# Latents before queries: another order of projections in a mixer, and a third query buffer

## The chip, the cores and the metric

The kernel runs on one core of a Trainium2 chip, in float32. The metric is the device time of one execution in microseconds; the median of several runs counts.

## The reference, cut to what matters

One inference step of a backbone with two layers, on 128 context tokens and 256 latent tokens of width 1024, plus 128 cached context tokens that the latent tokens may read. Layer 0 has mixers A and B, layer 1 has mixers C and D; each is followed by a SwiGLU FFN. The change is in layer 1 alone:

```
cq, ckv, kpe, qd, kd, vd = split(h @ w_in, (384, 256, 32, 512, 256, 256))
qc  = rms_norm(cq) @ w_q_up                  # 8 heads x (64 + 32)
ckv = rms_norm(ckv)
qd, kd = rms_norm per head                   # 8 and 4 heads x 64
kc, vc = split(ckv @ w_kv_up), kpe joined to kc
oc = softmax(qc kc^T) vc                     # mixer C, 8 heads
od = softmax(qd kd^T) vd                     # mixer D, 8 heads on 4 kv heads
y  = concat(oc, od) @ w_out
```

Context tokens read themselves only; latent tokens read latent and cached tokens, with a rotation of queries and keys.

## The kernel before, in words

Tokens form three tiles of 128. The normed and modulated input of a layer lies transposed in SBUF as a high and a low part (`hH`, `hL`), and each weight is split likewise: ScalarE rounds it (`wh`, L122), VectorE subtracts (`wl`, L123). A product is then three matmuls (`mm3`, L127 to L129). `proj_all` projects all three tiles: its weights come in four quarters of 256 rows, and each quarter takes one of three raw buffers and one of three split buffers, in the order of the program.

PSUM has eight banks in this stage: four in the pool `ps` (`pst`), three in `pj` (`pjt`), one apart (`psa`). A projection of three tiles takes three banks. Projections of D's keys and values (columns 1184 to 1695 of `w_in`, begun in the boundary behind the FFN of layer 0 and handed over as `acc0`), of C's query latents (0 to 383) and of C's key/value latents with the rotated key (384 to 671) go to `pj`; that of D's queries (672 to 1183) goes to `ps`, where the attentions' scores go, too. The banks of `pj` also hold the transposes of keys (`tk`), of C's query latents (`tc`) and of its key latents (`tl`), and the expansions (`vn`, `kn` in `kv_up`; `qu`, `tqc` in `q_up`).

What empties the banks: `evac_dkv` squares the keys on ScalarE (L1274), sums on VectorE (L1276), takes the power -1/2 on GpSimd (L110), and the product L1287 is the last read of the bank. `evac_cq` copies and squares a tile's latents (L1354, L1355), transposes, scales and splits them; it uses two working buffers `u2` of three. `evac_dq` squares, rotates and transposes D's queries into `qD`, a buffer of kind `qS`; `q_up` writes its two halves into two more buffers of that kind, of which there are two.

The order is made by a list scheduler when the program is built: each instruction has its place in the program as its priority, and `with ahead(name)` moves that place forward by `AHEAD[name]` instructions, or back if the number is negative. Engines then take what is ready by priority. Loads of weights carry a lead of 1500. In the program, layer 1's mixer is: project D's queries; empty keys and values (`evac_dkv`); cached keys (`d_ctx`); empty D's queries; C's query latents (200 back); C's cached latents and key/value latents (400 back); `kv_up` (30 ahead); D's attention (100 ahead); `q_up` (1000 ahead); C's attention (400 ahead); the first half of the output projection (1500 ahead). An attention has five stages (the context tokens, then four pairs of heads), and a stage's scores and exponentials stand ahead of the weighted sums of the stage before.

Of the kernel before, what the change touches and what calls it, by code (L numbers as in the profile page):

```python
# [28 lines left out]

AHEAD = {"w": 1500, "w0": -700, "lv0": 1000, "lv1": 800, "attA": 1500, "attC": 400, "attD": 100, "fin": 500, "qs": -1500,  # L30
         "ada": -400, "ada_step": -500, "of0": -500, "of1": 1500, "ho0": 300, "ho1": 300, "gb": 100, "ib": -60,
         "kvup": 30, "cq": -200, "dctx": -100, "lat": -400, "chain": -700, "qup": 1000, "rope": 1000, "adav": -500,
         "of2": -200, "adav1": -100}

ADA = (([(0, 2), (0, 3), (0, 4)], [(0, 5, 0), (1, 0, 1), (1, 1, 0), (1, 2, 1), (1, 3, 0), (1, 4, 1)]), ([], [(1, 5, 0)]))
# [6 lines left out]
def tile_backbone_step(ctx, tc, I, O):  # L42
# [33 lines left out]
    @contextmanager  # L76
    def ahead(part, more=0):
        with tc.high_priority(offset=AHEAD[part] + more):
            yield
# [271 lines left out]
    def tok(t):  # L351
        return slice(t * P, (t + 1) * P)
# [3 lines left out]
    def proj_parts(src, n, bank=None):  # L356
        acc, ws = {}, {}

        def load(u, *a, **kw):
            ws[u] = wload(src(slice(u * 256, (u + 1) * 256)), 2, n, *a, **kw)  # L360

        def part(t, u):
            if t not in acc:
                acc[t] = (bank or pjt)(f"pj{t}")
            hi, lo = ws[u]
            for k in range(2):
                kk = 2 * u + k
                mm3(acc[t][:, :n], hH[:, kk, tok(t)], hL[:, kk, tok(t)], hi[:, k, :], lo[:, k, :],
                    kk == 0, kk == KD - 1)

        return acc, part, load

    def proj_all(w, c0, n, bank=None):
        acc, part, load = proj_parts(lambda ks: w[ks, c0:c0 + n], n, bank)
        for u in range(4):
            load(u)
            for t in range(3):
                part(t, u)
        return acc

    def proj_tm(w, c0, n, evac):
        acc = proj_all(w, c0, n)
        for t in range(3):
            evac(t, acc[t])
# [233 lines left out]

    def inv_sums(M, A, sm, nm, sink, n):
        if A.sink:  # L620
            es = M.sm.tile([P, n], F32, tag=f"es{n}", name="es")
            nc.vector.tensor_tensor(out=es.rearrange("p (a b) -> p a b", a=2), in0=nm, in1=sink, op=ALU.add)
            nc.scalar.activation(es, es, AF.Exp)
            nc.vector.tensor_tensor(out=sm, in0=sm, in1=es, op=ALU.add)
        rd = M.sm.tile([P, n], F32, tag=f"rd{n}", name="rd")
        nc.vector.reciprocal(out=rd, in_=sm)
        return rd


    def pair_1(M, i, A):  # L630
        pr = [M.tile("pr", F32).rearrange("p (t k) -> p t k", t=2) for _ in range(2)]
        mx = M.sm.tile([P, 2, 2], F32, tag="mx", name="mx")
        sm = M.sm.tile([P, 4], F32, tag="sm", name="sm")
        nm = M.sm.tile([P, 2, 2], F32, tag="nm", name="nm")
        heads = slice(2 * i, 2 * i + 2)
        for qt in range(2):
            s_ = [pst("s")[:, :NTOK] for _ in range(2)]
            A.s(s_, i, qt)
            for a in range(2):
                nc.vector.tensor_reduce(out=mx[:, qt, a:a + 1], in_=s_[a], op=ALU.max, axis=AX.X)  # L640
            neg_max(A, nm[:, qt], mx[:, qt], heads, 1 + qt)
            for a in range(2):
                nc.scalar.activation(pr[a][:, qt, :], s_[a], AF.Exp, bias=nm[:, qt, a:a + 1],
                                     scale=score_scale(A, 2 * i + a, 1 + qt),
                                     accum_out=sm[:, 2 * qt + a:2 * qt + a + 1])
        sink = C["sink"][:, heads].unsqueeze(1).to_broadcast([P, 2, 2]) if A.sink else None
        rd = inv_sums(M, A, sm, nm, sink, 4)
        for qt in range(2):
            for a in range(2):
                nc.gpsimd.tensor_scalar(out=pr[a][:, qt, :], in0=pr[a][:, qt, :],  # L650
                                        scalar1=rd[:, 2 * qt + a:2 * qt + a + 1], scalar2=1.0, op0=ALU.mult, op1=ALU.mult)
        return pr

    def evac(eng, out, in_):
        if eng:
            nc.vector.tensor_copy(out=out, in_=in_)
        else:
            nc.scalar.activation(out, in_, AF.Copy)
# [86 lines left out]
    def rope_apply(M, x, nh, hd, tab, tt, dst, dup, tag="t2"):  # L745
        q = hd // 4
        t2f = M.tile(tag, F32)[:, 0:nh * hd].rearrange("p (h d) -> p h d", h=nh)
        xv = x.rearrange("p h (b k q) -> p h b k q", b=2, k=2)
        t2 = t2f.rearrange("p h (b k q) -> p h b k q", b=2, k=2)
        sv = tab[:, tt, 1, :].rearrange("p (b k q) -> p b k q", b=2, k=2)  # L750
        for k in range(2):
            nc.gpsimd.tensor_tensor(out=t2[:, :, :, k, :], in0=xv[:, :, :, 1 - k, :],
                                    in1=sv[:, :, k, :].unsqueeze(1).to_broadcast([P, nh, 2, q]), op=ALU.mult)
        nc.vector.tensor_tensor(out=x, in0=x, in1=tab[:, tt, 0, :].unsqueeze(1).to_broadcast([P, nh, hd]), op=ALU.mult)
        if dup:
            for d, sl in dst:
                n = sl.stop - sl.start
                nc.vector.tensor_tensor(out=d, in0=x[:, sl].unsqueeze(2).to_broadcast([P, n, 2, hd]),
                                        in1=t2f[:, sl].unsqueeze(2).to_broadcast([P, n, 2, hd]), op=ALU.add)
        else:  # L760
            nc.vector.tensor_tensor(out=dst, in0=x, in1=t2f, op=ALU.add)


    def dups(M, nh):
        r = []
        for h0 in range(0, nh, 4):
            n = min(4, nh - h0)
            r.append((M.tile("t2", F32)[:, 0:n * P].rearrange("p (h a d) -> p h a d", h=n, a=2), slice(h0, h0 + n)))
        return r
# [19 lines left out]
    def turn_k(ds, kT, tk, bank=pst):  # L789
        for d, sl in ds:  # L790
            n = sl.stop - sl.start
            tp = bank("tk").rearrange("p (h t) -> p h t", h=4)
            for i in range(n):
                nc.tensor.transpose(tp[:, i, :], d[:, i].rearrange("p a d -> p (a d)"), ident)
            for i in range(0, n, 2):
                evac(i, kT[i // 2][:, :, tk], tp[:, i:i + 2, :])
# [443 lines left out]
    def mixer_cd(ps1, acc0):  # L1240
        w = I["w_in_cd"][0]
        SC_D = 64 ** -0.5
        SC_C = 96 ** -0.5
        es = ExitStack()
        M = Slots(es, {"m4": (4, 1152), "u2": (3, 512), "t2": (5, 512), "one": (1, 0), "m8": (3, 2048), "qS": (2, 1536),
                       "pr": (4, 768), "pt": (6, 512), "sc": (1, 0)})
        vD = M.one.tile([P, 4, 4, 64], F32, name="vD")
        scl = {}
# [16 lines left out]
        def d_ctx():  # L1265
            kcx = dups(M, 4)
            for i in range(2):
                dma(out=kcx[0][0][:, :, i, :], in_=I["cache_d_k"][0, 0])
            dma(out=vD[:, 3], in_=I["cache_d_v"][0, 0])
            turn_k(kcx, kD, slice(384, 512), pjt)  # L1270

        def head_ss(acc, nh):
            sq = M.tile("t2", F32)[:, 0:nh * 64].rearrange("p (h d) -> p h d", h=nh)
            nc.scalar.activation(sq, acc.rearrange("p (h d) -> p h d", h=nh), AF.Square)  # L1274
            ss = M.sm.tile([P, 8], F32, tag="ssd", name="ssd")
            nc.vector.tensor_reduce(out=ss[:, :nh], in_=sq, op=ALU.add, axis=AX.X)  # L1276
            return ss
# [17 lines left out]
        def evac_dq(t, acc):  # L1295
            qn = M.tile("t2", F32).rearrange("p (h d) -> p h d", h=8)
            nc.scalar.activation(qn, acc.rearrange("p (h d) -> p h d", h=8), AF.Copy)
            ss = head_ss(acc, 8)
            if t:
                rope_apply(M, qn, 8, 64, tbq, t - 1, qn, False)  # L1300
            else:
                nc.vector.tensor_tensor(out=qn, in0=qn, in1=C["gdq"].unsqueeze(1).to_broadcast([P, 8, 64]), op=ALU.mult)
            turn_q(qn, qD, tok(t))
            with ahead("qs"):
                query_scale("D", t, ss, 1.0 / 64, SC_D)
# [115 lines left out]
        kT = [t8(F32, f"kT{i}") for i in range(2)]  # L1421
        latH, latL = [M.tile("m4", F32R)[:, 0:1024].rearrange("p (k n) -> p k n", k=2) for _ in range(2)]
        cqH, cqL = [M.tile("m4", F32R).rearrange("p (k n) -> p k n", k=3) for _ in range(2)]
        acc1 = proj_all(w, 672, 512, pst)
        for t in range(3):
            evac_dkv(t, acc0[t])
        d_ctx()
        for t in range(3):
            evac_dq(t, acc1[t])
        with ahead("cq"):  # L1430
            proj_tm(w, 0, 384, evac_cq)
        with ahead("lat"):
            c_ctx_()
            proj_tm(w, 384, 288, evac_ckv)
        with ahead("kvup"):
            vC = kv_up()
        with ahead("attD"):
# [98 lines left out]
```

## Time and profile before

| | us |
|---|---|
| median of 3 runs | 1082.47 |
| lowest, highest | 1077.73, 1084.74 |
| the profiled execution | 1080.16 |
| its span, first to last instruction | 1078.3 |
| TensorE busy | 1023.6 (95%) |
| VectorE busy | 657.7 (61%) |
| ScalarE busy | 440.5 (41%) |
| GpSimd busy | 121.2 (11%) |

The span and all rows below are of the profiled execution, which lies 1.9 us above its span and 2.3 below the median. In the rows PE is TensorE's matmuls, PEld its weight loads, DVE VectorE, ACT ScalarE, POOL GpSimd, SP the queue that issues the DMAs; L with a number is a line of the kernel. An operation is written as output<-inputs. In rows of time, the first number is the start in us from the span's start, the second how long it took; idle time ahead of it and what ended it stand in brackets.

### The profile page before, as it was taken

The page shows a single profiled execution, that of the slowest core. Times are in us where ns is not written, and L with a number is a line of the kernel's source. Part 1 is how long each engine was busy: PE and PEld are TensorE (multiplying, and loading weights), DVE is VectorE, ACT ScalarE, POOL GpSimd, SP SyncE. Part 2 cuts the span into 40 slices and gives each one's busy share as a digit, 9 for nine tenths or more (in the row PEclk, how much of TensorE's full clock was granted, in tenths as well). Part 3 has the DMA queues.
Part 4 walks back from the last instruction along what each step waited for, and adds up shares of the span by engine and source line. Part 5 has one row for each costly group of instructions (what it writes and reads, how often), then busy time and mean ns, then how long its engine had stood idle before and what let it go on. Part 6 is the DMA issues. An engine that isn't in the chain of part 4 may idle for free.

```text
span 1078.3 us, 15811 instructions
## 1 busy us (share of the span) xinstructions
PE 1023.6 (95%) x6105; PEld 865.2 (80%) x6105; DVE 657.7 (61%) x1110; ACT 440.5 (41%) x776; POOL 121.2 (11%) x166
## 2 busy tenths in 40 slices
PE   5999999997899999999999998979899999999995
PEld 4889877565799899897688776665689999998885
DVE  2589767455897477377247867656499464443337
ACT  2376746333443333232134457555163333332231
POOL 0021201210300000000001243122130000000004
PEclk8999999999999999999999999989999999999998
DMA  9873254457257777766663621144136464543331
GB/s 306 261 229 96 84 194 148 128 166 254 79 176 229 262 205 234 233 202 224 219 198 105 188 66 61 34 156 157 40 114 198 122 192 137 164 129 129 126 117 59
DMA packets 114353, 173.12 MB, mean 161 GB/s; under 512 B 9419, under 2 KB 82150, under 8 KB 114278
## 3 DMA queue, kind: packets, MB, share of 16 engines
q1 hardware_dynamic: 113526, 171.78, 50.7%
q8 instruction: 48, 0.79, 0.3%
q10 hardware_dynamic: 752, 0.34, 0.1%
q14 instruction: 27, 0.22, 0.1%
HBM read 167.84 MB, written 4.24 MB: 160 GB/s over the span
## 4 chain that ended last, share of the span: by engine, by line
PE 75%; DVE 9%; DMA 8%; issue 3%; ACT 2%; POOL 2%; SPq 0%; DVEq 0%; ACTq 0%; POOLq 0%
PE pf L129 10%; PE pf L128 10%; PE pf L127 10%; PE o L127 6%; PE o L128 6%; PE o L129 6%; DMA ar<-in_w_ada 4%; PE pj L129 3%; PE pj L127 3%; PE pj L128 3%; PE ada_acc L203 3%; DVE wl L123 2%; PE hs L883 2%; PE s L722 2%; PE ov L679 1%
## 5 line engine op out<-in xcount | busy, mean ns | idle before, releaser
L123 DVE TENSOR_TENSOR wl<-wr,wh 128x1024 fp32r<-128x1024 f32 (+4 forms) x200 | 235.9, 1182 | 239.9 <-ACT wh L122 237.1
L122 ACT ACTIVATE wh<-wr 128x1024 fp32r<-128x1024 f32 (+4 forms) x200 | 202.4, 1015 | 345.0 <-PE pf L128 123.5
L129 PE MATMUL pf<-hH,wl 128*128 128x384 f32 x688 | 232.7, 338 | 0.0
L127 PE MATMUL pf<-hH,wh 128*128 128x384 f32 x688 | 232.4, 338 | 0.0
L128 PE MATMUL pf<-hL,wh 128*128 128x384 f32 x688 | 232.4, 338 | 0.0
L129 PEld LDWEIGHTS pf<-hH,wl 128*128 128x128 f32 x688 | 129.4, 188 | 3.1 <-issue 3.1
L128 PEld LDWEIGHTS pf<-hL,wh 128*128 128x128 f32 x688 | 129.4, 188 | 2.5 <-issue 2.5
L127 PEld LDWEIGHTS pf<-hH,wh 128*128 128x128 f32 x688 | 129.4, 188 | 2.3 <-issue 2.2
L127 PE MATMUL o<-wh,aH 128*128 128x512 f32 (+1 forms) x280 | 101.3, 362 | 0.4 <-DVE a L1182 0.4
L128 PE MATMUL o<-wl,aH 128*128 128x512 f32 (+1 forms) x280 | 101.2, 361 | 0.4 <-DVE wl L123 0.4
L129 PE MATMUL o<-wh,aL 128*128 128x512 f32 (+1 forms) x280 | 101.0, 361 | 0.0
L129 PE MATMUL pj<-wh,hL 128*128 128x512 f32 (+3 forms) x240 | 88.9, 372 | 1.9 <-POOL hL L344 1.7
L127 PE MATMUL pj<-wh,hH 128*128 128x512 f32 (+3 forms) x240 | 89.2, 376 | 0.4 <-DVE vT L174 0.2
L261 DVE SCALAR_TENSOR_TENSOR part<-ar,cT,part 128x512 f32<-128x512 f32 x112 | 80.4, 747 | 13.7 <-DMA ar<-in_w_ada 13.6
L128 PE MATMUL pj<-wl,hH 128*128 128x512 f32 (+3 forms) x240 | 88.7, 370 | 0.0
L110 POOL TENSOR_TENSOR ve<-ve,nhalf 128x1 f32<-128x1 f32 x12 | 7.0, 585 | 631.7 <-DVE ve L530 370.2
L127 PEld LDWEIGHTS o<-wh,aH 128*128 128x128 f32 x280 | 52.9, 189 | 10.1 <-issue 1.4
L129 PEld LDWEIGHTS o<-wh,aL 128*128 128x128 f32 x280 | 52.8, 188 | 9.2 <-issue 1.2
L128 PEld LDWEIGHTS o<-wl,aH 128*128 128x128 f32 x280 | 52.9, 189 | 8.8 <-DVE wl L123 0.7
L129 PEld LDWEIGHTS pj<-wh,hL 128*128 128x128 f32 x240 | 45.1, 188 | 12.0 <-POOL hL L344 2.6
L127 PEld LDWEIGHTS pj<-wh,hH 128*128 128x128 f32 x240 | 44.8, 188 | 9.7 <-issue 1.9
L128 PEld LDWEIGHTS pj<-wl,hH 128*128 128x128 f32 x240 | 45.2, 188 | 7.8 <-issue 1.0
(325 smaller groups left out, 1511.5 us busy)
## 6 DMA issues: line engine op xcount, KB each, us to landing
ar<-in_w_ada SPq DMA_DIRECT2D x80, 512.0 KB
wr<-in_w_ffn_down SPq DMA_DIRECT2D x44, 512.0 KB
wr<-in_w_ffn_gate SPq DMA_DIRECT2D x40, 512.0 KB
wr<-in_w_ffn_up SPq DMA_DIRECT2D x40, 512.0 KB
wr<-in_w_in_ab SPq DMA_DIRECT2D x18, 512.0 KB
ar<-in_w_ada SPq DMA_DIRECT2D x32, 256.0 KB
wr<-in_w_out SPq DMA_DIRECT2D x16, 512.0 KB
wr<-in_w_in_ab SPq DMA_DIRECT2D x16, 256.0 KB
```

The costliest lines, as they stand in the source:

```text
L110: nc.gpsimd.tensor_tensor(out=out, in0=v, in1=nhalf[:, :n], op=ALU.pow)
L122: nc.scalar.activation(hi, raw, AF.Copy)
L123: nc.vector.tensor_tensor(out=lo, in0=raw, in1=hi.bitcast(F32), op=ALU.subtract)
L127: nc.tensor.matmul(out, lh, rh, start=start, stop=False)
L128: nc.tensor.matmul(out, lh, rl, start=False, stop=False)
L129: nc.tensor.matmul(out, ll, rh, start=False, stop=stop)
L203: nc.tensor.matmul(acc[32 * g:32 * g + 32], st, src[:, :, g * P:(g + 1) * P], start=start, stop=stop, tile_position=(0, 32 * g))
L261: nc.vector.scalar_tensor_tensor(out=dst, in0=raw[:, j], scalar=sc, in1=dst, op0=ALU.mult, op1=ALU.add)
L679: nc.tensor.matmul(ov[64 * a:64 * a + 64], A.v(kc + 1, 2 * i + a), pt[a, kc], start=(kc == 0), stop=(kc == 2))
L722: nc.tensor.matmul(outs[a], q[rows], k[rows], start=True, stop=stop)
L883: nc.tensor.matmul(pp[:, b, :], Kc(b0 + b), Qc(b0 + b), start=True, stop=True)
```

## The change

The projection of D's queries and what follows from it (`d_ctx`, `evac_dq`) move behind C's two projections; C's projections lose the numbers that moved them back; and buffers of kind `qS` become three. Calls of the two attentions stay one after the other.

```diff
-         "kvup": 30, "cq": -200, "dctx": -100, "lat": -400, "chain": -700, "qup": 1000, "rope": 1000, "adav": -500,
+         "kvup": 30, "cq": 0, "dctx": -100, "lat": 0, "chain": -700, "qup": 1000, "rope": 1000, "adav": -500,
...
-        M = Slots(es, {"m4": (4, 1152), "u2": (3, 512), "t2": (5, 512), "one": (1, 0), "m8": (3, 2048), "qS": (2, 1536),
+        M = Slots(es, {"m4": (4, 1152), "u2": (3, 512), "t2": (5, 512), "one": (1, 0), "m8": (3, 2048), "qS": (3, 1536),
...
-        acc1 = proj_all(w, 672, 512, pst)
         for t in range(3):
             evac_dkv(t, acc0[t])
-        d_ctx()
-        for t in range(3):
-            evac_dq(t, acc1[t])
         with ahead("cq"):
             proj_tm(w, 0, 384, evac_cq)
         with ahead("lat"):
             c_ctx_()
             proj_tm(w, 384, 288, evac_ckv)
+        acc1 = proj_all(w, 672, 512, pst)
+        d_ctx()
+        for t in range(3):
+            evac_dq(t, acc1[t])
         with ahead("kvup"):
             vC = kv_up()
```

## Rows read from the trace of the kernel before

**Rows 1.** The chain that ended last, shares of the span by engine.

```profile
PE 75%; DVE 9%; DMA 8%; issue 3%; ACT 2%; POOL 2%; SPq 0%; DVEq 0%; ACTq 0%; POOLq 0%
```

**Rows 2.** Stretches: width; busy of PE, PEld, DVE, ACT, POOL; clock; DMA; GB/s.

```profile
608.00:625.00 17.00, 17.00 (x76) 13.69 (x75) 11.68 (x23) 4.79 (x9) 5.80 (x7) 1.00 0.63 196
625.00:637.00 12.00, 10.47 (x68) 10.20 (x67) 9.56 (x23) 6.61 (x15) 8.04 (x7) 1.00 0.19 48
637.00:693.00 56.00, 50.26 (x324) 36.59 (x323) 38.05 (x90) 36.96 (x102) 17.15 (x28) 1.00 0.16 49
693.00:714.00 21.00, 18.86 (x104) 16.38 (x104) 12.02 (x24) 9.95 (x18) 3.22 (x8) 1.00 0.33 112
714.00:723.00 9.00, 5.15 (x19) 4.17 (x20) 6.37 (x11) 4.26 (x13) 1.71 (x1) 0.62 0.58 192
723.00:753.00 30.00, 29.48 (x143) 17.86 (x141) 16.87 (x34) 16.91 (x42) 9.92 (x14) 1.00 0.47 158
753.00:771.00 18.00, 14.94 (x79) 9.92 (x79) 4.45 (x9) 6.70 (x16) 2.27 (x4) 1.00 0.01 1
```

**Rows 3.** TensorE's waits, 607 to 772: total us, times, longest.

```profile
PE tqc L1405 <- DVE nm L613: 3.4, 1, 3.4
...
PE tqc L1405 <- DVE u L761: 1.6, 2, 0.8
...
PE s L1416 <- DVE qS L1406: 1.0, 1, 1.0
```

**Rows 4.** Stretches of 2 us where the granted clock (last but two) is low.

```profile
716.00:718.00 2.00, 0.00 (x0) 0.00 (x0) 2.00 (x5) 0.00 (x0) 0.00 (x0) 0.50 0.81 250
...
722.00:724.00 2.00, 2.00 (x8) 1.58 (x8) 0.12 (x1) 2.00 (x11) 0.00 (x0) 0.82 0.43 123
```

**Rows 5.** TensorE in time: first and last of 21, 30 and 18 matmuls.

```profile
619.78 0.40 PE L127 MATMUL pj<-wh,hH 128*128 128x512 f32 x1
...
624.45 0.40 PE L129 MATMUL pj<-wh,hL 128*128 128x512 f32 x1
...
629.14 0.34 PE L127 MATMUL pj<-wh,hH 128*128 128x384 f32 x1
...
634.27 0.34 PE L129 MATMUL pj<-wh,hL 128*128 128x384 f32 x1
...
656.21 0.38 PE L127 MATMUL pj<-wh,hH 128*128 128x288 f32 x1
...
658.54 0.29 PE L129 MATMUL pj<-wh,hL 128*128 128x288 f32 x1
```

**Rows 6.** ScalarE, GpSimd and VectorE in time: emptying D's keys.

```profile
605.29 0.38 ACT L1274 ACTIVATE t<-pj 128x256 f32<-128x256 f32 x1 [0.34 <-PE pj L129]
...
610.09 1.37 POOL L110 TENSOR_TENSOR rds<-ssd,nhalf 128x4 f32<-128x4 f32 x1 [12.29 <-DVE ssd L1232]
...
611.49 0.42 DVE L1287 TENSOR_TENSOR t<-pj,rds 128x256 f32<-128x256 f32 x1 [0.30 <-POOL rds L110]
...
616.26 0.42 DVE L1287 TENSOR_TENSOR t<-pj,rds 128x256 f32<-128x256 f32 x1 [1.13 <-POOL rds L110]
...
621.25 0.43 DVE L1287 TENSOR_TENSOR t<-pj,rds 128x256 f32<-128x256 f32 x1 [1.19 <-POOL rds L110]
```

**Rows 7.** Last matmul of C's query latents; the stretch behind it.

```profile
644.94 0.34 PE L129 MATMUL pj<-wh,hL 128*128 128x384 f32 x1
...
645.00:656.00 11.00, 7.69 (x47) 4.15 (x45) 10.26 (x27) 8.53 (x25) 6.74 (x9) 1.00 0.32 109
```

**Rows 8.** TensorE in time: the first scores of D.

```profile
637.38 1.80 PE L722 MATMUL s<-k,qS 64*128 64x128 f32 x18
```

**Rows 9.** TensorE in time: D's last scores, C's first query expansion.

```profile
671.76 1.56 PE L722 MATMUL s<-k,qS 64*128 64x384 f32 x8
...
697.14 0.33 PE L127 MATMUL qu<-wh,m 128*128 128x384 f32 x1
```

**Rows 10.** The DMA queue in time: first weights of that expansion.

```profile
668.23 2.62 SPq L118 DMA_DIRECT2D wr<-in_c_w_q_up x2
```

## The prediction

> **What bounds the kernel now.** I read the chain that ended last first: three quarters of the span lie on TensorE [rows 1], so a change pays only where it removes or creates idle TensorE time, or time at the low clock. Next comes the table of stretches over the second mixer [rows 2], from the end of the projection of D's keys and values (about 608 us) to just behind the last weighted sum of C's attention (771 us). Width less PE busy is what is left to win: 0, 1.53, 5.74, 2.14, 3.85, 0.52 and 3.06 us, together 16.8 us. The table of TensorE's waits names the largest: three steps between C's query projection and the start of C's attention, 3.4 + 1.6 + 1.0 = 6.0 us [rows 3]. VectorE is the cause: it is splitting weights and turning queries while a transpose waits at the head of TensorE's queue. The granted clock then stands at 0.50 (1.2 GHz, the lower of its two levels) from 716 us into the stretch that begins at 722 [rows 4]. TensorE works from 719 to about 722.5 at that level, so some 1.7 us are lost on top. All slack of the mixer is thus 18.5 us, 1.7% of the span.
>
> **The cost of the moved pieces.** From the starts of first and last of a row of back-to-back matmuls [rows 5]: 512 columns take 4.67/20 = 0.234 us, 384 take 5.13/29 = 0.177, 288 take 2.33/17 = 0.137. Hence D's queries (72) 16.8 us, C's query latents (72) 12.7, C's key/value latents (72) 9.9, the expansion of keys and values (48 of 512) 11.2, and of C's queries (54 of 384) 9.6 and 24 transposes. No work is added or removed; the sum is over gaps alone. D's queries end at 624.7 and take 16.8, so the keys and values of D end at 607.9.
>
> **1. From D's keys and values to C's query latents.** Both sit in the same three PSUM banks (pj); D's queries sit in the other pool. Today the 16.8 us of D's queries cover the emptying of these banks. After the change the next matmuls are C's latents, and D's queries can't step in: weights go through three buffers in program order, and theirs now come behind eight loads of C. So TensorE waits for the first bank. Today the multiplication that reads a bank last starts at 611.49, 616.26 and 621.25 for the three token tiles and lasts 0.42 [rows 6]. At that pace: 4.0 us idle to 611.9, then 3.2 us of work (three of four weight quarters, 18 matmuls of 384), 1.6 idle, 3.2 work, 1.8 idle: 7.4 us. The lower bound is the chain by itself: the square starts at 605.29 and ScalarE is free for the next tile at once [rows 6]; with VectorE free, square, sum, power on GpSimd (1.37) and product would end some 3 us later, 0.7 us after 607.9. But VectorE is finishing the previous layer's output there, whose instructions are unchanged. I take 4.5 us: nearer to today's rows for the first bank, faster for the others, since ScalarE's square of the second tile waits today behind a weight split that after the change can't come before it. The key transposes, which use a bank each too, lie inside this.
>
> **2. From C's query latents to its key/value latents.** Again the same three banks. Today 11 us lie between the last matmul of the one, just before 645.2, and the first of the other at 656.21 [rows 5, 7]; TensorE fills 7.69 us of them with D's attention [rows 7]. After the change there is no attention yet. Bounds: 0, if the banks turn over under the latents' own last matmuls, and 10 us, if today's distance stays with only the transposes in it. ScalarE is 8.53 us busy there [rows 7], more than half of it with exponentials that are now absent. But the latents of each tile occupy two of three working buffers, so the tiles go one after another. I take 4 us.
>
> **3. From D's queries to its attention.** D's first score stands at 637.38 [rows 8], 12.7 us after the projection; today C's latents cover this. The expansion of keys and values, 11.2 us, takes over: its inputs have been ready for the whole of D's queries. Cost 0 to 2, taken 0.5. The 1.53 us wait for the cached keys (the idle time of 625 to 637 [rows 2]) goes under the same cover: -1.5. If the expansion were not ready, up to all 12.7 us would lie bare.
>
> **4. C's queries and the start of its attention.** Their expansion carries a lead of 1000 in the priority list, yet today it runs only at 697.14 [rows 9], since its weights come last in the queue (668.23 [rows 10]). After the change its latents are ready about 17 us before D's attention begins; its weights follow those of keys and values directly, so it runs inside D's attention, C's scores are ready before D ends, and the 6.0 + 1.7 us go. Here the third buffer counts: D's queries hold one slot, C's two halves need two, and with two slots the second half would wait for D's last score (671.76 today [rows 9], much later after). Today that slot is free some 24 us before it is wanted, so the buffer without the new order would gain nothing: taken -7.7, bounds -7.7 and 0.
>
> A rule of the Trainium skill (Perfetto Trace Analysis, Identifying Performance Opportunities) says that consistent bubbles can mean too little SBUF or PSUM for the next tile. Read for the query buffers, it would credit the 7.7 us to the third buffer alone; rows 9 speak against that. Read for the PSUM banks of steps 1 and 2, it speaks against this change, and no stretch of before shows it, because the banks have cover there.
>
> **5. D's attention itself** loses C's two projections as filler and gets C's expansion, and early parts of C's attention, whose priority then overlaps with D's last stages. Its 5.74 us of idle time [rows 2] I set at 4.5: -1.2, bounds -4 and +5. The last 3.06 us before 771 stay. If the wait of step 1 is as long as the 3.4 us of rows 3, the low clock follows it as there: +1.7, bounds 0 and 3.5 (once for each of steps 1 and 2).
>
> **Sum.** +4.5 + 4 + 0.5 - 1.5 - 7.7 - 1.2 + 1.7 = +0.3 us. The profiled execution took 1080.16 us (span 1078.3 and 1.9 around it), which makes 1080.5; it lies 2.3 below the median of the runs, from which the sum gives 1082.8. I forecast between the two: **1081.5 us**, no change.
>
> **Rivals.**
> - *The banks decide (slower).* Steps 1 and 2 cost their upper bounds, 7.4 + 10, step 3 costs 2 and the clock drops twice (3.5): 22.9 - 1.5 - 7.7 - 1.2 = +12.5, 1093 to 1095. For it: three banks, one user after the other, no other matmul with weights at hand. Against: most of today's delay there comes from work that has moved away. It is slower by over 1% when idle time and low clock between 608 us and D's queries cost more than about 20 us.
> - *The evacuations are quick and the two attentions fill each other (faster).* Steps 1 and 2 cost 0.7 and 1, no clock drop, D's attention 2 us: 0.7 + 1 - 1.5 - 7.7 - 3.7 = -11.2, about 1070. For it: ScalarE is idle most of 608 to 625 (4.79 of 17 us [rows 2]). Against: VectorE is busy 11.68 of those 17.
> - *The order moves, the bubble does not.* VectorE, the cause of the 3.4 us, still splits the output weights when C's queries end, or they come no earlier. Then +0.3 + 7.7 = +8, 1089: still within 1%.
> - *Regimes pulled apart.* D's attention keeps only C's query expansion as filler, and TensorE waits as often as it does without projections: the 714 to 771 stretches idle 7.4 us in 57 [rows 2], so over D's 56 us 7.3 in place of 4.5, +2.8, and the cover of step 3 is missing by some 3 us: +6, 1087. The Trainium skill (Perfetto Trace Analysis, Optimization Strategy) advises interleaving stretches whose most-contended engine differs; before does that with projections and D's attention, and the change undoes part of it. Its stretch of 637 to 693 idles 10%, so the trace bears the rule out only in part.
>
> **How the numbers follow.** Forecast 0.42, banks 0.20, quick 0.14, bubble stays 0.13, regimes 0.11. The forecast's case spreads over some 7 us to either side. One per cent, 10.8 us, is about what a measurement of this kernel can tell from no change. Slower by over 1%: most of the bank case and a little of the two before 1089, 0.20. Faster by over 1%: most of the quick case, 0.13. The rest, 0.67, is within. The range takes in most of the quick and of the bank case: 1068 to 1095.
>
> **What would show it.** Right: a gap of TensorE of 3 to 5 us at 608 that ends with the product of D's keys (L1287), a second gap before the matmuls of 288 columns, the query expansion (qu) inside D's scores, no wait of its transposes (tqc) over 1 us. Wrong: the first gap under 1 us, or over 7 in pieces; qu behind D's last weighted sum; or a new gap before D's first score, which would say that keys and values were not ready.

## The result and the profile after

The changed kernel takes 1098.21 us (median of 4 runs, 1094.64 to 1099.99) against 1082.16 for the kernel before on the same chip: ratio 1.0138, 95% interval 1.0109 to 1.0168. It is slower by 1.4%, above the forecast of 1081.5 and outside the range of 1068 to 1095. The profiled execution took 1099.73 us (span 1097.9) against 1080.16.

The chain that ended last still lies on TensorE, with a little more on VectorE and DMA than in [rows 1]:

```profile
PE 74%; DVE 10%; DMA 9%; issue 3%; ACT 2%; POOL 1%; SPq 0%; ACTq 0%; DVEq 0%; POOLq 0%
```

The stretches of the second mixer, cut where the new order changes its work; the last runs from the first expansion of C's queries to the end of the output projection (columns as in [rows 2]: width, busy of PE, PEld, DVE, ACT, POOL, granted clock, DMA share, GB/s):

```profile
609.00:624.50 15.50, 3.22 (x14) 2.19 (x13) 8.80 (x21) 2.50 (x7) 5.13 (x7) 0.62 0.43 137
624.50:638.20 13.70, 13.70 (x76) 13.67 (x75) 3.06 (x5) 3.97 (x8) 0.47 (x1) 0.93 0.20 48
638.00:644.30 6.30, 1.93 (x14) 1.25 (x12) 4.48 (x15) 3.69 (x9) 1.37 (x3) 0.94 0.61 183
...
655.20:672.00 16.80, 16.80 (x75) 13.50 (x73) 8.51 (x18) 7.12 (x14) 2.58 (x6) 1.00 0.50 157
672.00:682.00 10.00, 7.12 (x35) 5.63 (x33) 8.62 (x23) 5.60 (x12) 8.49 (x9) 0.83 0.07 21
...
695.40:808.10 112.70, 106.54 (x570) 72.85 (x568) 68.26 (x133) 55.27 (x133) 27.96 (x48) 0.97 0.28 93
```

In the first, between D's keys and values and C's query latents, TensorE works 3.22 us of 15.50: 12.3 idle, where the stretch of 608 to 625 in [rows 2] has none. Behind the query latents (638 to 644.3) 4.4 us are idle, behind D's queries (672 to 682) 2.9.

TensorE's waits from 600 to 800 us (total us, times, longest):

```profile
PE tk L794 <- DVE t L758: 7.6, 2, 4.2
PE tk L794 <- ACT t L778: 4.7, 1, 4.7
PE tl L1318 <- DMA u<-in_cache_c_kv: 3.0, 1, 3.0
PE pt L673 <- ACT pr L643: 2.4, 2, 2.2
PE tl L1318 <- DVE u L1340: 2.4, 1, 2.4
```

None of the three waits of [rows 3] is left. In their place the transposes of D's keys (tk) wait 12.3 us in three pieces, those of C's latents (tl) 5.4. TensorE in time (start, duration, in brackets the idle time ahead and its releaser):

```profile
608.86 0.39 PE L129 MATMUL pj<-wh,hL 128*128 128x512 f32 x1
...
613.98 1.11 PE L794 MATMUL tk<-ident,t 128*128 128x128 f32 x4 [4.73 <-ACT t L778]
...
619.25 1.09 PE L794 MATMUL tk<-ident,t 128*128 128x128 f32 x4 [4.16 <-DVE t L758]
...
623.74 1.12 PE L794 MATMUL tk<-ident,t 128*128 128x128 f32 x4 [3.40 <-DVE t L758]
624.50 0.67 PE L127 MATMUL pj<-wh,hH 128*128 128x384 f32 x1
...
643.98 0.66 PE L1318 MATMUL tl<-ident,u 128*128 128x128 f32 x2 [2.98 <-DMA u<-in_cache_c_kv]
```

All three groups of key transposes stand ahead of the first matmul of C's query latents (624.50). No wait of that matmul's own is shown; it stands behind the transposes in the queue. (Taking what is ready by priority is what the planner does while it writes the program; in the traces TensorE keeps to the order so written. With another written order, below, the latents start at 610.30.) Why the three tiles come one after another shows in GpSimd, VectorE and ScalarE over the same time:

```profile
610.50 1.37 POOL L110 TENSOR_TENSOR rds<-ssd,nhalf 128x4 f32<-128x4 f32 x1 [11.50 <-DVE ssd L1232]
...
611.91 0.42 DVE L1287 TENSOR_TENSOR t<-pj,rds 128x256 f32<-128x256 f32 x1 [0.30 <-POOL rds L110]
...
612.85 0.42 DVE L1290 TENSOR_TENSOR t<-t,gdk 128x256 f32<-128x256 f32 x1
...
613.30 0.63 ACT L778 ACTIVATE t<-t 128x512 f32<-128x512 f32 x1 [6.14 <-DVE t L1290]
613.83 0.37 ACT L1274 ACTIVATE t<-pj 128x256 f32<-128x256 f32 x1
...
614.23 0.42 DVE L1276 TENSOR_REDUCE ssd<-t 128x4 f32<-128x256 f32 x1 [0.97 <-ACT t L1274]
```

ScalarE stands 6.14 us at the copy that doubles tile 0's keys (L778), and the square of tile 1 (L1274) is queued behind it. The banks' last readers (L1287) run at 611.91, 616.50 and 621.13, the pace of [rows 6].

### The profile page after: what moved, and what is told of

It is laid out like the page before. It is cut to its first block, busy times and chain, and to the rows that moved or that the text cites. A ratio compares the mean times of both kernels' runs of the same rounds, so it can differ in the third digit from the quotient of the medians.

```text
span 1097.9 us, 15808 instructions
## 1 busy us (share of the span) xinstructions
PE 1034.5 (94%) x6105; PEld 871.7 (79%) x6105; DVE 656.7 (60%) x1110; ACT 442.7 (40%) x776; POOL 116.2 (11%) x166
## 4 chain that ended last, share of the span: by engine, by line
PE 74%; DVE 10%; DMA 9%; issue 3%; ACT 2%; POOL 1%; SPq 0%; ACTq 0%; DVEq 0%; POOLq 0%
PE pf L129 9%; PE pf L128 9%; PE pf L127 9%; PE o L127 7%; PE o L128 6%; PE o L129 6%; DMA ar<-in_w_ada 6%; PE pj L127 4%; PE pj L129 4%; PE pj L128 4%; PE ada_acc L203 3%; DVE wl L123 2%; PE s L722 2%; PE hs L883 2%; DVE part L261 2%
## 5 line engine op out<-in xcount | busy, mean ns | idle before, releaser
L261 DVE SCALAR_TENSOR_TENSOR part<-ar,cT,part 128x512 f32<-128x512 f32 x112 | 80.3, 746 | 13.2 <-DMA ar<-in_w_ada 12.9
L127 PE MATMUL o<-wh,hH 128*128 128x512 f32 (+1 forms) x112 | 44.8, 403 | 8.1 <-DVE x L520 3.9
```

What stands on the lines that cost most here:

```text
L127: nc.tensor.matmul(out, lh, rh, start=start, stop=False)
L261: nc.vector.scalar_tensor_tensor(out=dst, in0=raw[:, j], scalar=sc, in1=dst, op0=ALU.mult, op1=ALU.add)
```

## The experiments

"pj" is the group of three PSUM banks that D's keys and values, C's two sets of latents and their transposes share; "ps" is the other group, which D's queries use. All ratios are to the kernel before, with 95% intervals. Theory A: what cost the time is that C's query latents now follow D's keys in pj. Banks are asked for in program order, so the key transposes take theirs first and stand at the head of TensorE's queue with nothing in front that could cover them. Theory B: the regimes were pulled apart, that is, projections and attention no longer fill each other's gaps. Theory C: it is the place of the key transposes in the queue alone, not the banks.

### C's query latents in the other banks

```diff
-            proj_tm(w, 0, 384, evac_cq)
+            proj_tm(w, 0, 384, evac_cq, pst)
```

(proj_tm hands the bank on to proj_all.)

> The changed kernel with one edit: C's query latents accumulate in the other PSUM pool (ps, free at that time) and no longer in the three banks that D's keys and values hold. Theory A (the banks lost their cover): TensorE's three waits for the key transposes at 609 to 624 us, 12.3 us, and the low clock behind them, some 2 us, go; about 1083 to 1086 us. Rival B (projections and attention pulled apart cost the time, the early gap would otherwise appear later): the idle time moves behind the latents, less than 5 us are won, 1093 us or more. Rival C (the place of the key transposes in TensorE's queue alone, whatever the banks): as A here, told apart by the next run.

Measured 1081.33 us, ratio 0.9976 (0.9958 to 0.9995): the whole loss is gone with one argument, in the new order. (Some 4.8 us of this come from another order of the attention that the planner wrote along with the edit; the last experiment separates them.) Its waits:

```profile
PE tk L794 <- DVE t L758: 3.2, 1, 3.2
PE tl L1318 <- DVE u L1340: 2.4, 1, 2.4
PE tl L1318 <- DMA u<-in_cache_c_kv: 2.3, 1, 2.3
```

12.3 us at the key transposes became 3.2: two thirds of C's query latents now run ahead of the first of them. B is out, since the order of projections and attentions is that of the changed kernel.

### The key transposes behind the query latents, banks as they were

```diff
+        ds = [evac_dkv(t, acc0[t]) for t in range(3)]
+        with ahead("cq"):
+            accq = proj_all(w, 0, 384)
         for t in range(3):
-            evac_dkv(t, acc0[t])
+            turn_k(ds[t], kD, tok(t), pjt)
...
```

evac_dkv gives back the keys here and turns nothing; turn_k makes the transposes; the emptying of C's query latents, left out here, follows them.

> The changed kernel with one edit: the key transposes of D's three tiles stand in the program behind the matmuls of C's query latents and not ahead of them; the banks are shared as before. Theory A: the latents now wait only for the product that reads each bank last (at about 612.3, 616.9 and 621.5 in the changed kernel), so 3.0 + 1.4 + 1.4 = 5.8 us of idle time stay of 12.3 and the low clock may go: 1090 to 1093 us. Rival C (place in the queue alone): as good as the other pool, 1083 to 1086. Rival B: 1093 or more.

Measured 1092.22, ratio 1.0085 (1.0058 to 1.0111). Its waits:

```profile
PE pj L127 <- DVE t L1287: 3.4, 2, 3.1
PE tk L794 <- DVE k L656: 3.0, 2, 2.1
```

The first matmul of the latents, in time:

```profile
610.30 0.44 PE L127 MATMUL pj<-wh,hH 128*128 128x384 f32 x1 [3.13 <-DVE t L1287]
```

Out of the queue's way, the latents wait for the banks themselves. The place in the queue is some 6 of the 16 us (both versions have the same order of attention); C alone is out.

### The old order with D's queries in pj

```diff
-        acc1 = proj_all(w, 672, 512, pst)
+        acc1 = proj_all(w, 672, 512)
```

This is the kernel before, with nothing moved, but the cover's banks taken from it.

> The old order, with one word taken out: D's query projection takes its banks from pj like D's keys, not from ps. Nothing is pulled forward, nothing is swapped, no buffer is added. Theory A (the cover of the key work is a matter of which banks the next projection takes): the key transposes now ask for their banks before D's queries do, stand ahead of them at TensorE's head, and a wait for t of 4 us or more appears between D's keys and D's queries, as in the changed kernel; idle time of TensorE grows by 4 to 7 us and some low clock comes with it: 1086 to 1091 us, ratio 1.004 to 1.008. Rival (what cost the changed kernel time is the swap of C's and D's projections, whatever the banks): 1080 to 1084, no new wait for t.

Measured 1088.38, ratio 1.0041 (1.0019 to 1.0063). The wait came, though at another place than the expectation said: the transposes stay behind D's queries, and the first matmul of these waits for its bank.

```profile
612.80 0.66 PE L127 MATMUL pj<-wh,hH 128*128 128x512 f32 x1 [3.92 <-DVE t L1287]
```

The swapped order loses nothing with a second group of banks (first experiment), and the old order loses 4 to 6 us without one: the second group was the cover that the kernel before had. How the loss of this run divides is not shown: the planner also wrote another order within D's attention here. Over the same work, from the end of D's keys and values to the end of the output projection, the kernel before and this run show

```profile
608.00:788.60 180.60, 163.38 (x913) 123.78 (x912) 114.25 (x236) 90.69 (x221) 51.97 (x74) 0.98 0.30 95
```

```profile
609.00:798.30 189.30, 171.15 (x912) 128.60 (x913) 113.23 (x236) 91.55 (x221) 49.71 (x74) 0.95 0.28 90
```

The idle time is 17.2 us in the first and 18.2 in the second, so the new wait of 3.9 is nearly made up for elsewhere; most of what this execution is longer by lies in busy time, at a mean clock of 0.95 in place of 0.98.

### Two buffers for queries; a third one in the old order

```diff
-  "qS": (3, 1536)      in the changed kernel
+  "qS": (2, 1536)
-  "qS": (2, 1536)      in the kernel before
+  "qS": (3, 1536)
```

> The changed kernel with two query buffers as before in place of three. My prediction gave the third buffer a part in the 7.7 us won at the start of C's attention: then this is slower than the changed kernel by 2 to 8 us. Rival: the slots are not what orders this stage, and it takes the same time within 1 us, 1098.

> The kernel before with a third buffer for queries and nothing else. If the waits of C's query transposes there (3.4 and 1.6 us) were for a buffer: they shrink and the time is 1078 to 1081. If they were for the chain on VectorE that makes the queries: 1081 to 1084, ratio 0.998 to 1.002, the waits as they were.

Two buffers in the changed kernel: 1097.30, ratio 1.0142 (1.0104 to 1.0179). Three in the kernel before: 1083.07, ratio 1.0003 (0.9982 to 1.0025), with the 3.4 us at tqc as it was. The third buffer makes no difference that can be measured in either order.

### Useless matmuls in the waits

```diff
...
+        fill = pat("fill")
         for t in range(3):
+            with tc.issue_after(C["pl"].ins if t == 0 else C["tk"].ins):
+                for _ in range((20, 17, 13)[t]):
+                    nc.tensor.matmul(fill[:, :NTOK], hH[:, 0, tok(0)], hH[:, 0, :], start=True, stop=True)
             evac_dkv(t, acc0[t])
```

C["pl"] and C["tk"] remember the last matmul of a product and the last key transpose. The unread matmuls stand behind the last matmul of D's keys and values and behind the first and the second group of key transposes.

> The changed kernel with 50 matmuls of 384 columns that nobody reads, 20, 17 and 13 of them ahead of the three key transposes, in the time in which TensorE waits for t; all its other work is as it was. They can't end a wait sooner. Theory A with the clock (the waits cost their own length and, beside that, the low clock behind them, worked out at some 4 to 5 us at this place): the spell of granted clock under 0.7 at 612.5 to 626 goes, and the time falls by 2 to 5 us, to 1093 to 1096, ratio to before 1.010 to 1.013. Rival (the low clock lies beside work that waits anyway and costs nothing): 1097 to 1099, and the first matmuls of C's query latents merely start later.

Measured 1097.23, ratio 1.0137 (1.0105 to 1.0169): A's figure missed, the rival's held. The clock stayed up as intended. The waits and then C's query latents, in the run with filling:

```profile
612.50:622.88 10.38, 6.94 (x43) 6.33 (x43) 4.92 (x12) 2.33 (x7) 3.78 (x6) 1.00 0.28 90
622.88:635.80 12.92, 12.92 (x77) 12.89 (x75) 3.00 (x5) 3.97 (x8) 0.46 (x1) 1.00 0.21 50
```

The clock is 1.00 where the changed kernel shows 0.62 and 0.93. The latents take 12.9 us where they took 13.7, and from the first transpose (613.02) to the first latent (622.88) 9.9 us pass where 10.5 did. So the low clock was worth 1.4 us at this place by the trace, not 4 to 5, and the median (1.0 us lower) can't tell that from nothing. A likely reason, not tested by itself, is that the transposes at the low clock lie in a chain whose pace VectorE and ScalarE set.

### A buffer of their own for C's cached latents

```diff
-  "sc": (1, 0)})
+  "sc": (1, 0), "lcx": (1, 288)})
-            lcx = M.tile("u2", F32)[:, 0:288]
+            lcx = M.tile("lcx", F32)
```

With the query latents in ps:

> The kernel with C's query latents in the other pool, and the cached latents of C read into a buffer of their own in place of one of three shared ones. The changed kernel waits 3.0 us for this read at 644 us and runs 10 matmuls at the low clock behind it. Theory A: another 3 to 4 us less than with the other pool alone, 1079 to 1083, at or a little under the kernel before. Rival B: no more than 1 us.

Measured 1078.85, ratio 0.9963 (0.9947 to 0.9980), 2.5 us below the run without, where A said 3 to 4; the two intervals overlap. In the changed kernel alone:

> The changed kernel with nothing but a buffer of their own for C's cached latents, so that their transfer needn't wait for a buffer of u2. In the changed kernel the latents' transposes waited 3.0 us for that transfer, and behind them the clock was low from 643.5 to 647. Banks account (each wait at TensorE's head between D's keys and D's queries is paid once): the wait of 3.0 goes and most of its low clock, 1094 to 1096 us, ratio to before 1.010 to 1.013. Rival (the wait is only hidden behind the next one, as the keys are late anyway): 1097 to 1099.

Measured 1091.69, ratio 1.0080 (1.0054 to 1.0106): 6.5 us for a wait of 3.0, twice what A said. Something else had moved.

### Taking the last key wait away

```diff
-            proj_tm(w, 384, 288, evac_ckv)
+            accl = proj_all(w, 384, 288)
+            for t in range(3):
+                turn_k(ds[t], kD, tok(t), pjt)
+            for t in range(3):
+                evac_ckv(t, accl[t])
...
-            tp = pjt("tl").rearrange("p (j t) -> p j t", j=4)
+            tp = pat("tl").rearrange("p (j t) -> p j t", j=4)
```

Two versions, the second of which alone has the last two lines (the latents' transposes in the spare bank). Both also have the query latents in ps and the own buffer of the cached latents.

> C's query latents in ps, the cached latents in a buffer of their own (both as in the run before that had them), and the three key transposes sent behind the matmuls of C's key latents. Theory A: the wait of 3.2 us for D's keys that was left between D's keys and C's query latents goes; what stays is the wait of the latents' transposes for u, 2 to 3 us, and the transposes' own 3 us: 1073 to 1078 us, ratio 0.991 to 0.996. Rival (the keys come later now, and D's first scores wait for the last of them, so the wait is only moved): 1078 to 1082, with a wait of 2 us or more at the scores or at tk.

> As the run beside it that sends the key transposes behind the matmuls of C's key latents, but the transposes of C's key latents take the spare bank of the attention's pool instead of one of pj. Theory A: a bank of pj comes free sooner and the wait of the transposes at u should lose up to 2.4 us if it was the bank's, nothing if it is u's own chain on VectorE: 1072 to 1078, within 2 us of the other. Rival: the spare bank is in use by the attention's own transposes, the latents' transposes fall behind them, and the time is 1 to 4 us above the other's.

> The fastest of the versions so far (C's query latents in ps, cached latents in a buffer of their own, key transposes behind C's key latents, latents' transposes in the spare bank) with two buffers for queries, not three. Here no wait is left ahead of the queries, so if the third buffer counts anywhere it is here. If it counts (C's queries are written while D's two halves are still read): a wait at tqc or s of 1 us or more and 1079 to 1083 us. If it doesn't: 1076 to 1079, ratio to before 0.995 to 0.998.

The first took 1081.22, ratio 0.9988 (0.9969 to 1.0006): A missed, and the rival too, since the time is its time but no wait of 2 us stands at the scores or at tk. The second took 1077.76, ratio 0.9962 (0.9942 to 0.9982): A's time, with no wait of the latents' transposes for u left, but 3.5 us from the first and not within 2 (the intervals overlap). With two query buffers it took 1079.35, ratio 0.9962 (0.9944 to 0.9980), with no wait of 1 us at tqc or s: the third buffer doesn't count here either. A wait of 3.2 us was gone, and neither version is clearly faster than the one with an own buffer before it (0.9963).

### One number of the planner's

What the two surprises share is TensorE's program behind D's first scores, which the planner writes out. It has two forms in these versions, and a third in the second version with late key transposes (tiles and counts, from the expansion of keys on, with scores between the first groups left out):

```
changed kernel, late keys: kn 6, pt, kn 6, pt, qu 3, s, ov, s, qu 5, ov, qu 19, ov, s ...
query latents in ps:      kn 12, pt, qu 3, s, qu 11, ov, s, ov, qu 13, ov, s ...
```

In the first the transposes of D's probabilities (pt) come too early and wait for pr. One number flips the form and leaves the order up to the first scores as it was:

```diff
-  "attD": 100     in the changed kernel
+  "attD": 20
-  "kvup": 30      in the first version with late key transposes
+  "kvup": 25
```

> The changed kernel with the planner's lead for D's attention at 20 where it was 100, which changes nothing of the order ahead of D's first scores and turns the order behind them into the one that the version with an own buffer for C's cached latents had. If that written order is worth the 3 to 5 us that the traces show between C's queries and the end of the attention (111 to 113 us against 108): 1093 to 1096 us, and the wait of 2.2 us of D's transposes for pr goes. If the stretch was only shifted by what came before it (the late transfer): 1097 to 1099, ratio to before 1.014 or above.

> The version with C's query latents in ps, the cached latents in their own buffer and the key transposes behind C's key latents (1081.2 us), with the planner's lead for the up-projection at 25 where it was 30: the order up to D's first scores stays, the order behind them becomes the other one. If the written order of the attention ate the wait that was removed: 1076 to 1079, ratio to before 0.994 to 0.997, 2 to 5 us under the version with the old order. If not: 1080 to 1082.

The changed kernel with the other form takes 1093.43, ratio 1.0096 (1.0069 to 1.0122), 4.8 us less. The stretch from C's first query expansion to the last weighted sum of C's attention, first in the changed kernel and in the changed kernel with the other form:

```profile
695.40:787.00 91.60, 87.51 (x463) 56.73 (x461) 52.02 (x107) 48.70 (x119) 24.22 (x42) 0.98 0.29 97
```

```profile
695.60:782.10 86.50, 83.58 (x463) 55.70 (x460) 52.37 (x106) 47.29 (x116) 26.06 (x42) 1.00 0.30 103
```

Then in the first version with late key transposes, and in that version with the other form:

```profile
678.50:769.90 91.40, 87.43 (x462) 56.80 (x460) 52.03 (x107) 48.72 (x119) 24.29 (x42) 0.98 0.28 97
```

```profile
678.90:765.60 86.70, 83.56 (x462) 55.65 (x460) 52.42 (x107) 47.98 (x120) 27.18 (x42) 1.00 0.31 102
```

In each pair the same work is shorter by some 5 us in the other form. About 1 of it is idle time; the rest is busy time, in which the worse form also has a spell of low clock (0.98 against 1.00).

The version with late key transposes becomes **1075.47 us, ratio 0.9926 (0.9901 to 0.9951)**: under both kernels, and the best measured. Of its waits for D's keys 0.9 us is left:

```profile
PE tl L1318 <- DVE u L1340: 1.7, 1, 1.7
...
PE tk L794 <- DVE k L656: 0.9, 1, 0.9
```

## Why the prediction was wrong

**What failed: step 1, by its size, and the size by a wrong cause.** I let the key transposes "lie inside this", took 4.5 us and bounded the step by 7.4, the pace at which the banks' last readers follow each other. It measured 12.3 us idle. The bound let C's latents enter each bank as it came free. But the key transposes ask for banks of pj first, they need the keys scaled, rotated and doubled behind that reader, and they go to TensorE first. So nothing of C could run between them. The reason I gave for tiles 1 and 2 going faster fell short as well. In the kernel before, the square of tile 1 stands on ScalarE behind a weight's rounding, but also behind the doubling of tile 0's keys:

```profile
612.29 1.06 ACT L122 ACTIVATE wh<-wr 128x1024 fp32r<-128x1024 f32 x1 [6.34 <-PE pj L129]
...
613.25 0.62 ACT L778 ACTIVATE t<-t 128x512 f32<-128x512 f32 x1
613.77 0.37 ACT L1274 ACTIVATE t<-pj 128x256 f32<-128x256 f32 x1
```

The change took the rounding away, the doubling stayed (it stands idle for 6.14 us until VectorE hands over tile 0), and the square came 1.9 us behind tile 0's product (L1287) where it had come 2.3 behind it. The experiments show the cause, not only its place: other banks for the latents take the loss away (12 of the 16 us, when the order of the attention is the same), the transposes sent later take some 6 of 16 us off, and the old order without its second group of banks gets a wait of 3.9 us and takes 4 to 6 us more (by ratio and by medians). The mark that I set for being wrong here, a gap of over 7 us in pieces, is what the profile shows.

**What failed besides: the low clock**, which I set at nothing on balance (-1.7 in step 4, +1.7 behind step 1). These are its spells in the changed kernel, and the one in the kernel before:

```profile
612.70:626.40 13.70, 4.87 (x18) 4.09 (x19) 5.82 (x15) 2.88 (x8) 3.75 (x6) 0.50 0.25 85
643.40:646.80 3.40, 2.83 (x12) 2.86 (x13) 0.15 (x3) 0.00 (x0) 0.00 (x0) 0.52 0.02 6
677.60:681.00 3.40, 3.40 (x9) 2.63 (x9) 3.01 (x8) 0.63 (x2) 2.97 (x4) 0.51 0.02 5
728.80:732.20 3.40, 3.40 (x10) 2.66 (x9) 0.18 (x1) 0.91 (x3) 2.27 (x4) 0.51 0.00 0
790.20:793.60 3.40, 3.23 (x8) 2.48 (x8) 2.35 (x5) 0.00 (x0) 0.00 (x0) 0.51 0.76 231
```

```profile
716.00:722.80 6.80, 3.79 (x10) 3.04 (x11) 4.37 (x9) 3.00 (x10) 0.00 (x0) 0.51 0.54 183
```

TensorE works 17.7 us at the lower level there and 3.8 before. In the changed kernel the matmuls of 512 columns at 678 us follow each other at 0.43 us, those at 685 at 0.23, so half of that time is lost at most: an estimate of 8.9 against 1.9 us. It is an upper bound, since the filled run took the first spell away and won 1.4 us at its place, not 2.4.

**Step 5 had no term for the order.** I set D's attention at -1.2 us because it would find other filler. Apart from step 4's 6.0 us and the 1.5 for the cached keys, the kernel before idles 9.7 us between the end of D's keys and values and the end of the output projection; apart from steps 1 to 3 the changed kernel idles 6.2. That is 3.5 less, but 3.4 of the 9.7 were waits at the transposes of C's latents (2.9 at tl, 0.5 at tc), which now stand in steps 2 and 3. The planner wrote another order behind D's first scores, and that order cost 4.8 us, as the run that flips it shows, most of it as busy time. I had no term for an order that is written anew wherever a finishing time moves.

**Step 2 was right**: 4 taken, 6.30 - 1.93 = 4.4 idle. Its reason was half right: 3.0 of it was the transfer of C's cached latents, which had to wait for a buffer of u2, and in the changed kernel with the good order that is worth some 1.7 us (1093.43 to 1091.69; the intervals overlap).

**Step 3**: 0.5 taken, 10.00 - 7.12 = 2.9 measured. The inputs of the expansion were not "ready for the whole of D's queries": the transposes of C's key latents came only behind D's queries, and one of them waited.

```profile
672.00 0.38 PE L1318 MATMUL tl<-ident,u 128*128 128x128 f32 x2
...
675.70 0.30 PE L1318 MATMUL tl<-ident,u 128*128 128x128 f32 x1 [2.44 <-DVE u L1340]
```

This is the gap before D's first score that I had named as a sign of being wrong. The wait for the cached keys is gone, as said (-1.5).

**Step 4 was right in its result and wrong on the buffer.** The 6.0 us of [rows 3] are gone, and so is the spell of low clock in [rows 4], and C's expansion runs inside D's scores:

```profile
695.42 0.42 PE L127 MATMUL qu<-wh,m 128*128 128x384 f32 x1
...
723.70 0.91 PE L722 MATMUL s<-k,qS 64*128 64x384 f32 x2
```

In [rows 9] it began 24 us behind D's last scores; here it begins 28 ahead of them. But two buffers do the same. The rule of the Trainium skill that I weighed there (Perfetto Trace Analysis, Identifying Performance Opportunities: consistent bubbles can mean too little SBUF or PSUM) is borne out for PSUM, some 12 us from the bank group alone (1093.43 to 1081.33, both with the same order of attention), and not for the query buffers (1.0003 with a third one).

**The sum with the measured terms.** Over the same work as in the row of 608 to 788.6 above, the changed kernel shows

```profile
609.00:808.10 199.10, 173.41 (x914) 129.24 (x912) 113.63 (x235) 93.27 (x221) 47.83 (x74) 0.93 0.28 88
```

The two profiled executions lie 18.5 us apart there (the medians of the runs 16.0). The idle time grew by 8.5 us: +12.3 + 4.4 + 2.9 - 1.5 - 6.0 - 3.5, but for rounding. The busy time grew by 10.0, of which the low clock makes up 7 at most; what the other 3 or more are is not shown. The 4.8 us of the planner's order lie within these figures and are not added to them. Of my +0.3, then, step 1 was 7.8 us too low and the clock up to 7.

The rival in which the banks decide had the mechanism and the sign. Its time, 1093 to 1095, came near in part by luck: it had 7.4 us for step 1, where 12.3 came, and 10 for step 2, where 4.4 came. That in which the regimes are pulled apart is refuted as the cause of the loss: with the latents in the other banks, the swapped order takes 0.9976 of the time before. The Trainium skill (Perfetto Trace Analysis, Optimization Strategy) says that interleaving such regimes may improve performance. These runs don't bear that out: with the projections gathered ahead of the attentions and the banks in order, the kernel is 0.7% faster than before. They do not refute it either, since the old order was not run with the same improvements.

## What to carry to other kernels

Before a projection is moved, list for each PSUM group who asks for its banks next, in program order: an early asker whose input is late holds up everything behind it in TensorE's queue, and a second group of banks is then a cover that no wait in the profile shows, because it works. Bound such a step by the whole chain up to the next asker's instruction, not by the banks' last reader. And where a planner writes the order, read the order of each version before a gain or a loss is put down to the edit: one of its numbers moved this kernel by 5 us.

## What the runs showed of the hardware

TensorE's clock fell to the lower level behind single waits of a few microseconds (2.98 us at 641 to 644; 0.79 over 639 to 647), and unread matmuls placed in the waits kept it at 1.00. Yet that brought 1.4 us at its place and nothing that the median could tell, while the next low stretch began earlier and lay deeper, at 0.54 where the changed kernel shows 0.80 over the same time:

```profile
639.00:646.50 7.50, 4.86 (x22) 4.79 (x23) 1.47 (x6) 0.83 (x3) 0.54 (x1) 0.54 0.25 82
```
